# Where the last gate's modulation weights are loaded, and how gathered rows are spread, in a transformer block with a product-key expert layer

## Chip, cores and metric

The kernel runs on one core of one Trainium2 chip. The metric is device microseconds of one execution; three executions were timed.

## The reference

One block with 256 tokens and model width 2048: attention and pooling first, then an expert layer with 16384 experts, of which every token uses 128 (8 heads, 16 each). All is float32. Cut to what matters here:

```python
mod = jax.nn.silu(c) @ ada_w[layer] + ada_b[layer]          # 2048 x 12288
shift1, scale1, gate1, shift2, scale2, gate2 = jnp.split(mod[:, None, :], 6, axis=-1)
...
xn2 = rms_norm(h, norm2_g[layer]) * (1.0 + scale2) + shift2
h = h + gate2 * peer_ffn(xn2, peer_wq, peer_keys, peer_down, peer_up)
return rms_norm(h, final_g)

def peer_ffn(xn, w_query, sub_keys, w_down, w_up):
    q = jnp.einsum('bsd,de->bse', xn, w_query).reshape(B, S, 8, 2, 128)
    s = jnp.einsum('bshpd,hpnd->bshpn', q, sub_keys)
    top_s, top_i = lax.top_k(s, 16)
    ...                                                   # 16 of 256 pairs: expert, gates
    u = jnp.take(w_down, ic, axis=0)
    a = jax.nn.gelu(jnp.einsum('cd,ced->ce', xc, u), approximate=False) * gc
    return jnp.einsum('ce,ced->cd', a, jnp.take(w_up, ic, axis=0))
```

The last sixth of `mod` is `gate2`. It is used only when the expert layer's output is added.

## The kernel before

The work is a list of steps, each with one block of weights of 128 x 2048 (two loads of 128 x 1024 float32, 512 KB). `run` (from L292) goes over the list and emits the program. Weights come through five raw buffers in a fixed order: `want` notes the loads, `fill` issues one on the SP queue as soon as a buffer has been given back, `take` and `give` hand a buffer out and return it. In most steps ScalarE copies a raw tile to a rounded high part (L158, hi), VectorE subtracts to get the low part (L164, lo), which gives the raw buffer back, and TensorE multiplies with both parts. `plan` places these splits about one and a half steps ahead of the matmuls.

The modulation is not a matmul. `ada_half` (L211) takes a raw tile of `ada_w`, multiplies it on VectorE with the broadcast of silu(c) and sums along the row; a column of 128 outputs takes two such tiles. Steps have a list `ada` of the tiles they handle; the loads stand in the same queue.

The stages that the change touches come in this order:

- **Query steps** (16, `wq`): high and low split, scores, and the top-16 search on VectorE. POOL writes the normalized input beside it.
- **First down layer** (half 0, 64 steps, `down`): the hidden values of the first 8192 experts, for all of the 192 tokens that are computed against every expert. These steps are exact: TensorE takes the raw tile itself (L346) and gives it back after its 8 matmuls; there is no split. The routing (`route`) runs beside the first 24 steps on VectorE, then the gate matmuls (L1043) run beside the rest.
- **First up layer** (half 0, 64 steps, `up`): the output sums, split again, 20 matmuls a step (L1124, L1126, L1128). Before the change its first 32 steps each handle one of the 32 `ada` tiles of `gate2` (columns 80 to 95).
- **Second down layer** and **second up layer** (half 1): 64 steps each, both split (L181, L182 for down). At the start of the second down layer, a reload of hT, a load of the gate table A, the gate row for `gate2` and the residual sum (L1224, L1225) run beside it.

The other 64 tokens have their 128 experts' rows gathered, in 64 gathers of `down` rows and 64 of `up` rows, 128 rows of 8 KB (1 MB) each: POOL issues the gather (L1162) into one of two row buffers, VectorE multiplies and sums (L1173) or adds (L1180), and only then the gather after the next is issued. `share` gives each of the last steps of the first down layer (from step RS = 24) and of the three following layers a weight, and the 128 row steps are spread by the running sum:

```python
share = [0.75] * (HB - RS) + [0.35] * 32 + [0.55] * (HB - 32) + [0.5] * HB + [0.55] * (HB - 4)
```

which makes 31 row steps in the first down layer, 29 in the first up layer (11 of them in its first half), 33 in the second down layer and 35 in the second up layer.

Of the kernel before, what the change touches and what calls it, by code (L numbers as in the profile page):

```python
# [20 lines left out]
KC = D // P  # L21
# [6 lines left out]
HB = NB // 2  # L28
# [3 lines left out]
RS = 24  # L32
# [61 lines left out]
def peer_block_kernel(ctx: ExitStack, tc, xT_d, c_d, cols_d, const_d, ada_d, gates_d, wide_d, blk_d, mix_d, br_d,  # L94
# [151 lines left out]
    steps = []  # L246
# [46 lines left out]
    def run():  # L293
        for n, parts in plan():
            acts = parts[0] + parts[1]
            if n >= 0 and steps[n].exact:
                pre = int(n >= 1 and parts[0] != [] and parts[0][0][0] == "half")
                acts[pre:pre] = [("half", steps[n], i) for i in range(2)]
            for a in acts:
                if a[0] == "ada":  # L300
                    want(ada_d[a[1]][:, a[2] * HW:(a[2] + 1) * HW], HW)
                elif a[0] == "half" and (a[2] == 0 or a[1].w == D):
                    w = min(a[1].w, HW)
                    want(a[1].src[:, a[2] * w:a[2] * w + w], w)
        want(fg_d.unsqueeze(0).to_broadcast([P, D]))
        for n, parts in plan():
            s = steps[n] if n >= 0 else None
            if n >= 1:
                first = parts[0][0] if parts[0] else None
                if first and first[0] == "half":  # L310
                    parts[0][0] = first + (split_hi(first[1], first[2]),)
                if steps[n - 1].evac:
                    steps[n - 1].evac()
            if s:
                s.mm(s.hs, s.ls, 0)
                side_step(0)
                s.mm(s.hs, s.ls, 1)
                s.hs, s.ls = None, None
            for a in parts[0]:
                act(a)  # L320
            while late:
                late.popleft()()
            for _ in range(s.rows if s else 0):
                sparse_step()
            if s:
                side_step(1)
                if s.tick:
                    s.tick()
            for a in parts[1]:
                act(a)  # L330
        if steps[-1].evac:
            steps[-1].evac()
# [156 lines left out]
    n0 = len(steps)  # L489
# [10 lines left out]
    n0 = len(steps)  # L500
# [595 lines left out]
    def up_step(half, bl, oc):  # L1096


        hs = half_state[half]
        st = {}  # L1100

        def prep():
            assert hs["g"] == NG
            src = hs["A"][bl // AB][:, :, bl % AB, :]
            a = pp["pk2"].tile([P, 2 * ND], F32R, tag="a2", bufs=3, name="a2")
            nc.scalar.copy(a[:, :ND].rearrange("p (g u) -> p g u", u=TG), src)
            for n0, n, o in ((0, P, P + 2 * SP), (P, SP, ND)):
                nc.vector.tensor_sub(a[:, o:o + n].rearrange("p (g u) -> p g u", u=TG), src[:, n0 // TG:(n0 + n) // TG],  # L1108
                                     a[:, n0:n0 + n].rearrange("p (g u) -> p g u", u=TG).bitcast(F32))
            st["a"] = a  # L1110

        def mm(h_, l_, part):
            if bl == 0 and part == 0:
                oc.extend(psum(f"oc{i}") for i in range(8))
            a, last = st["a"], half == 1 and bl == HB - 1
            if last and part == 0:
                return

            def go(q, t, low):
                o, c = oc[2 * q + t], slice((q % 2) * 512, (q % 2 + 1) * 512)  # L1120
                w = (l_ if low else h_)[q // 2][:, c]
                st_, sp_ = bl == 0 and not low, low and bl == HB - 1
                if t:
                    nc.tensor.matmul(o, a[:, P:P + 2 * SP], w, start=st_, stop=sp_)  # L1124
                else:
                    nc.tensor.matmul(o, a[:, :P], w, start=st_, stop=sp_)  # L1126
                    if not low:
                        nc.tensor.matmul(o, a[:, P + 2 * SP:], w, start=False, stop=False)  # L1128

            if last:  # L1130
                order = [(q, t, low) for t in (1, 0) for q in range(4) for low in (False, True)]
            else:
                order = [(q, t, low) for low in (False, True) for q in (2 * part, 2 * part + 1) for t in range(2)]
            for o in order:
                go(*o)

        return Step(up_d[half * HB + bl], mm, after=[prep],
                    ada=[(80 + bl // 2, bl % 2)] if half == 0 and bl < 32 else [])

# [88 lines left out]
    for half in range(2):  # L1230
        n0 = len(steps)
        for bl in range(HB):
            steps.append(block_step(down_d[half * HB + bl], x2act if half else lambda k: x2f[:, k, :],
                                    lambda ps, half=half, bl=bl: h_done(half, bl, ps), both=half == 1, exact=half == 0))
        if half == 0:
            steps[n0 + 2].tick = open_late

            steps[n0 + 5].tick = lambda: side.append(gate_groups())
# [8 lines left out]
    steps[n0 + 24].tick = lambda: load_gates(NA - 1)  # L1247


    share = [0.75] * (HB - RS) + [0.35] * 32 + [0.55] * (HB - 32) + [0.5] * HB + [0.55] * (HB - 4)  # L1250
    total, seen = sum(share), 0.0
    for i, w in enumerate(share):
        n = int(seen / total * 2 * NP + 1e-6)
# [100 lines left out]
```

## Time and profile before

| | us |
|---|---|
| median of 3 executions | 2128.38 |
| lowest and highest | 2125.85, 2128.86 |
| profiled execution | 2129.82 |
| its span | 2127.9 |
| TensorE busy in the span | 1998.6 (94%) |
| VectorE busy in the span | 1683.0 (79%) |
| mean granted TensorE clock | 0.975 of 2.4 GHz |

The span is what the trace covers; the execution's own time is 1.9 us longer. Durations below come from this one execution. A busy share is a mean over stages with different limits, so a stage has to be read by itself. Issue to landing is the time from the instruction that issues a transfer to the semaphore that says it has landed.

### The profile page before, as it was taken

The page shows a single profiled execution, that of the slowest core. Times are in us where ns is not written, and L with a number is a line of the kernel's source. Part 1 is how long each engine was busy: PE and PEld are TensorE (multiplying, and loading weights), DVE is VectorE, ACT ScalarE, POOL GpSimd, SP SyncE. Part 2 cuts the span into 40 slices and gives each one's busy share as a digit, 9 for nine tenths or more (in the row PEclk, how much of TensorE's full clock was granted, in tenths as well). Part 3 has the DMA queues.
Part 4 walks back from the last instruction along what each step waited for, and adds up shares of the span by engine and source line. Part 5 has one row for each costly group of instructions (what it writes and reads, how often), then busy time and mean ns, then how long its engine had stood idle before and what let it go on. Part 6 is the DMA issues. An engine that isn't in the chain of part 4 may idle for free.

```text
span 2127.9 us, 33391 instructions
## 1 busy us (share of the span) xinstructions
PE 1998.6 (94%) x12444; PEld 1840.0 (86%) x12444; DVE 1683.0 (79%) x2908; ACT 900.9 (42%) x1473; POOL 368.4 (17%) x384
## 2 busy tenths in 40 slices
PE   7899999999999999999998878999689999999994
PEld 5889998999999999999996656878689999888883
DVE  8987887889888774577767767887588899888886
ACT  3344554544545411122224334454345556454553
POOL 2101231111216300111110000111111121332220
PEclk8999999999999999999999989999799999999997
DMA  9997877878986466899999999999879999999993
GB/s 373 380 341 259 317 266 246 283 276 311 316 306 197 143 205 200 315 324 319 329 331 317 310 318 328 372 360 351 254 268 334 349 354 359 350 359 353 352 362 112
DMA packets 171973, 648.83 MB, mean 305 GB/s; under 512 B 21025, under 2 KB 30529, under 8 KB 155041
## 3 DMA queue, kind: packets, MB, share of 16 engines
q1 hardware_dynamic: 147568, 499.18, 66.5%
q0 software_dynamic: 19200, 136.87, 17.5%
q10 hardware_dynamic: 5042, 10.64, 1.3%
q8 instruction: 98, 1.61, 0.3%
q14 instruction: 65, 0.53, 0.1%
HBM read 636.13 MB, written 10.49 MB: 304 GB/s over the span
## 4 chain that ended last, share of the span: by engine, by line
PE 62%; DMA 12%; DVE 9%; issue 4%; ACT 3%; POOL 0%; SPq 0%; DVEq 0%; ACTq 0%; POOLq 0%
PE blk L346 15%; PE oc L1124 8%; PE oc L1126 8%; PE blk L181 7%; DMA raw<-in_up_dram 7%; PE blk L175 4%; PE blk L176 4%; PE blk L174 4%; PE oc L1128 4%; DVE lo L164 3%; PE blk L182 3%; DMA raw<-in_blk_dram 2%; PE gps L1043 2%; ACT hi L158 2%; DVE raw L211 1%
## 5 line engine op out<-in xcount | busy, mean ns | idle before, releaser
L158 ACT CAST hi<-raw 128x1024 fp32r<-128x1024 f32 (+1 forms) x602 | 613.1, 1026 | 597.6 <-DMA raw<-in_up_dram 213.1
L164 DVE TENSOR_TENSOR lo<-raw,hi 128x1024 fp32r<-128x1024 f32 (+1 forms) x602 | 717.5, 1202 | 143.0 <-ACT hi L158 136.1
L346 PE MATMUL blk<-hT,raw 128*128 128x192 f32 x2048 | 338.0, 326 | 0.0
L346 PEld LDWEIGHTS blk<-hT,raw 128*128 128x128 f32 x2048 | 332.1, 190 | 0.5 <-issue 0.3
L181 PE MATMUL blk<-xn,hi 128*128 128x384 f32 x1024 | 302.2, 367 | 9.7 <-ACT hi L158 9.0
L182 PE MATMUL blk<-xn,lo 128*128 128x192 f32 x1024 | 260.6, 254 | 18.2 <-DVE lo L164 18.2
L211 DVE SCALAR_TENSOR_TENSOR raw<-raw,cb 128x1024 f32<-128x1024 f32 x165 | 213.0, 1309 | 40.5 <-DMA raw<-in_ada_dram 40.4
L1126 PE MATMUL oc<-hi,a 128*128 128x512 f32 x512 | 206.6, 404 | 33.2 <-ACT hi L158 33.2
L182 PEld LDWEIGHTS blk<-xn,lo 128*128 128x128 f32 x1024 | 199.2, 194 | 20.6 <-DVE lo L164 20.6
L1128 PE MATMUL oc<-hi,a 128*128 128x512 f32 x512 | 205.8, 402 | 4.8 <-DVE a L1108 4.7
L1124 PE MATMUL oc<-hi,a 128*128 128x512 f32 x512 | 205.5, 401 | 1.4 <-ACT hsum L1077 1.4
L1126 PE MATMUL oc<-lo,a 128*128 128x512 f32 x512 | 206.1, 403 | 0.0
L181 PEld LDWEIGHTS blk<-xn,hi 128*128 128x128 f32 x1024 | 195.9, 191 | 11.6 <-ACT hi L158 10.4
L1124 PE MATMUL oc<-lo,a 128*128 128x512 f32 x512 | 204.7, 400 | 0.0
L1162 POOL DMA_INDIRECT rows<-in_up_dram,spidx x64 | 125.5, 1962 | 441.9 <-DVE a L1108 200.1
L1162 POOL DMA_INDIRECT rows<-in_rows_dram,spidx x64 | 64.3, 1005 | 674.1 <-DVE a L1108 329.1
L1173 DVE SCALAR_TENSOR_TENSOR rows<-rows,rows 128x2048 f32<-128x2048 f32 x64 | 146.2, 2284 | 11.1 <-DMA rows<-in_rows_dram,spidx 11.1
L1126 PEld LDWEIGHTS oc<-hi,a 128*128 128x128 f32 x512 | 97.9, 191 | 61.5 <-ACT hi L158 38.5
L1180 DVE SCALAR_TENSOR_TENSOR rows<-rows,sph,rows 128x2048 f32<-128x2048 f32 x63 | 147.7, 2345 | 1.9 <-DMA rows<-in_up_dram,spidx 1.9
L174 PE MATMUL blk<-xna,hi 128*128 128x256 f32 x480 | 138.7, 289 | 0.0
L176 PE MATMUL blk<-xna,lo 128*128 128x256 f32 x480 | 135.8, 283 | 0.0
L175 PE MATMUL blk<-xna,hi 128*128 128x256 f32 x480 | 135.7, 283 | 0.0
(296 smaller groups left out, 3750.2 us busy)
## 6 DMA issues: line engine op xcount, KB each, us to landing
raw<-in_down_dram SPq DMA_DIRECT2D x256, 512.0 KB, 6.8
raw<-in_up_dram SPq DMA_DIRECT2D x256, 512.0 KB, 7.6
raw<-in_ada_dram SPq DMA_DIRECT2D x165, 512.0 KB, 5.8
raw<-in_blk_dram SPq DMA_DIRECT2D x80, 512.0 KB, 5.6
raw<-in_wout_dram SPq DMA_DIRECT2D x32, 512.0 KB, 5.9
raw<-in_wq_dram SPq DMA_DIRECT2D x32, 512.0 KB, 4.0
xraw<-in_ada_dram SPq DMA_DIRECT2D x27, 512.0 KB, 6.4
raw<-in_gates_dram SPq DMA_DIRECT2D x23, 512.0 KB, 5.7
```

The costliest lines, as they stand in the source:

```text
L158: nc.scalar.copy(hi, r)
L164: nc.vector.tensor_sub(lo, r, s.hs[i].bitcast(F32))
L174: nc.tensor.matmul(out, wh, ah, start=start, stop=False)
L175: nc.tensor.matmul(out, wh, al, start=False, stop=False)
L176: nc.tensor.matmul(out, wl, ah, start=False, stop=stop)
L181: nc.tensor.matmul(ps[:, :2 * ND], wh, a.rearrange("p s n -> p (s n)"), start=start, stop=False)
L182: nc.tensor.matmul(ps[:, :ND], wl, a[:, 0, :], start=False, stop=stop)
L211: nc.vector.scalar_tensor_tensor(raw, raw, 1.0, cb[:, i * HW:(i + 1) * HW], op0=ALU.mult, op1=ALU.mult, accum_out=modp[:, i, m:m + 1])
L346: nc.tensor.matmul(st["ps"][:, :ND], raw[:, c], a, start=k == 0, stop=k == KC - 1)
L1124: nc.tensor.matmul(o, a[:, P:P + 2 * SP], w, start=st_, stop=sp_)
L1126: nc.tensor.matmul(o, a[:, :P], w, start=st_, stop=sp_)
L1128: nc.tensor.matmul(o, a[:, P + 2 * SP:], w, start=False, stop=False)
```

## The change

It makes three edits. The 32 `ada` tiles of `gate2` move from the first 32 steps of the first up layer to the last 12 query steps and the first 20 steps of the first down layer, one a step. In exact steps the step's own two loads now always come first in the load order, and the early high-part split that came before them is left out there. And `share` has other weights: the first down layer now has 38 row steps, the first up layer 30, the second down layer 26 and the second up layer 34.

```diff
--- before.py
+++ after.py
@@ -294,8 +294,7 @@
         for n, parts in plan():
             acts = parts[0] + parts[1]
             if n >= 0 and steps[n].exact:
-                pre = int(n >= 1 and parts[0] != [] and parts[0][0][0] == "half")
-                acts[pre:pre] = [("half", steps[n], i) for i in range(2)]
+                acts[:0] = [("half", steps[n], i) for i in range(2)]
             for a in acts:
                 if a[0] == "ada":
                     want(ada_d[a[1]][:, a[2] * HW:(a[2] + 1) * HW], HW)
@@ -307,7 +306,7 @@
             s = steps[n] if n >= 0 else None
             if n >= 1:
                 first = parts[0][0] if parts[0] else None
-                if first and first[0] == "half":
+                if first and first[0] == "half" and not (s and s.exact):
                     parts[0][0] = first + (split_hi(first[1], first[2]),)
                 if steps[n - 1].evac:
                     steps[n - 1].evac()
@@ -1134,8 +1133,7 @@
             for o in order:
                 go(*o)
 
-        return Step(up_d[half * HB + bl], mm, after=[prep],
-                    ada=[(80 + bl // 2, bl % 2)] if half == 0 and bl < 32 else [])
+        return Step(up_d[half * HB + bl], mm, after=[prep])
 
 
 
@@ -1233,6 +1231,8 @@
             steps.append(block_step(down_d[half * HB + bl], x2act if half else lambda k: x2f[:, k, :],
                                     lambda ps, half=half, bl=bl: h_done(half, bl, ps), both=half == 1, exact=half == 0))
         if half == 0:
+            for m in range(2 * KC):
+                steps[n0 - 12 + m].ada.append((80 + m // 2, m % 2))
             steps[n0 + 2].tick = open_late
 
             steps[n0 + 5].tick = lambda: side.append(gate_groups())
@@ -1247,7 +1247,7 @@
     steps[n0 + 24].tick = lambda: load_gates(NA - 1)
 
 
-    share = [0.75] * (HB - RS) + [0.35] * 32 + [0.55] * (HB - 32) + [0.5] * HB + [0.55] * (HB - 4)
+    share = [0.95] * (HB - RS) + [0.47] * HB + [0.42] * HB + [0.55] * (HB - 4)
     total, seen = sum(share), 0.0
     for i, w in enumerate(share):
         n = int(seen / total * 2 * NP + 1e-6)
```

The changed program's line numbers are one lower from L299 on, two lower from L1138 on, and the same again from L1236 on.

**SP, the load queue, from the query steps on.** Before, the queue has all query loads, all down loads, and then one modulation tile after every two up loads:

```order
L132 DMA raw<-in_wq_dram 128x1024 x32
L132 DMA raw<-in_down_dram 128x1024 x126
L132 DMA raw<-in_up_dram 128x1024 x2
L132 DMA raw<-in_down_dram 128x1024 x2
L132 DMA raw<-in_up_dram 128x1024 x2
L132 DMA raw<-in_ada_dram 128x1024
L132 DMA raw<-in_up_dram 128x1024 x2
L132 DMA raw<-in_ada_dram 128x1024
L132 DMA raw<-in_up_dram 128x1024 x2
L132 DMA raw<-in_ada_dram 128x1024
```

After, from the last query steps into the first down layer:

```order
L132 DMA raw<-in_wq_dram 128x1024 x2
L132 DMA raw<-in_ada_dram 128x1024
L132 DMA raw<-in_wq_dram 128x1024 x2
L132 DMA raw<-in_ada_dram 128x1024 x2
L132 DMA raw<-in_down_dram 128x1024 x2
L132 DMA raw<-in_ada_dram 128x1024
L132 DMA raw<-in_down_dram 128x1024 x2
L132 DMA raw<-in_ada_dram 128x1024
L132 DMA raw<-in_down_dram 128x1024 x2
L132 DMA raw<-in_ada_dram 128x1024
L132 DMA raw<-in_down_dram 128x1024 x2
```

One modulation tile stands behind every two weight tiles from query step 4 to down step 19, and none in the up layer.

**SP, the up layer.** Before, around the first gate-table load (A):

```order
L132 DMA raw<-in_ada_dram 128x1024
L132 DMA raw<-in_up_dram 128x1024 x2
L132 DMA raw<-in_ada_dram 128x1024
L132 DMA raw<-in_up_dram 128x1024 x2
L1010 DMA A<-g2d 128x24x168
L132 DMA raw<-in_ada_dram 128x1024
L132 DMA raw<-in_up_dram 128x1024 x2
L132 DMA raw<-in_ada_dram 128x1024
L132 DMA raw<-in_up_dram 128x1024 x2
```

After, from the last modulation tile to the second gate-table load:

```order
L132 DMA raw<-in_ada_dram 128x1024
L132 DMA raw<-in_down_dram 128x1024 x86
L132 DMA raw<-in_up_dram 128x1024
L132 DMA raw<-in_down_dram 128x1024 x2
L132 DMA raw<-in_up_dram 128x1024 x52
L1009 DMA A<-g2d 128x24x168
L132 DMA raw<-in_up_dram 128x1024 x42
L1009 DMA A<-g2d 128x24x168
L132 DMA raw<-in_up_dram 128x1024 x33
```

The up loads run without anything between them but the two gate tables, and one up load stands before the last two down loads instead of two.

**VectorE, the routing of the second 64 tokens in the first down layer** (four, cp, tif, gz and e are routing tiles). Before, from the second top-16 search to the wait for ScalarE's exponential at gz:

```order
L860 MAX_INDEX cp<-four,tmpc 128x8 x4
L852 MAX four<-cand 128x8 x4
L854 MAX_INDEX cp<-four,cand 128x8 x4
L856 MATCH_REPLACE tmpc<-four,cand 128x50 x4
L858 MAX four<-tmpc 128x8 x4
L860 MAX_INDEX cp<-four,tmpc 128x8 x4
L933 TENSOR_TENSOR four<-four 128x128
L935 CAST four<-cp 128x128
L936 CAST tif<-tops 128x256
L937 COPY four<-tif 128x8
L938 TENSOR_TENSOR four<-tif 128x8x15
L941 TENSOR_REDUCE gz<-four 128x8
```

After, the same piece:

```order
L211 SCALAR_TENSOR_TENSOR raw,modp<-raw,cb 128x1024
L851 MAX four<-cand 128x8 x4
L853 MAX_INDEX cp<-four,cand 128x8 x4
L855 MATCH_REPLACE tmpc<-four,cand 128x50 x4
L857 MAX four<-tmpc 128x8 x4
L859 MAX_INDEX cp<-four,tmpc 128x8 x4
L932 TENSOR_TENSOR four<-four 128x128
L934 CAST four<-cp 128x128
L935 CAST tif<-tops 128x256
L936 COPY four<-tif 128x8
L937 TENSOR_TENSOR four<-tif 128x8x15
L211 SCALAR_TENSOR_TENSOR raw,modp<-raw,cb 128x1024
```

The modulation multiplies (L211) stand between the pieces of the routing, in program order.

## Rows read from the trace of the kernel before

**Rows 1.** The page: busy us by engine, then TensorE busy and clock in 40 slices.

```profile
PE 1998.6 (94%) x12444; PEld 1840.0 (86%) x12444; DVE 1683.0 (79%) x2908; ACT 900.9 (42%) x1473; POOL 368.4 (17%) x384
...
PE   7899999999999999999998878999689999999994
...
PEclk8999999999999999999999989999799999999997
```

**Rows 2.** Stretches: window, length, busy us (instructions) by engine, clock, DMA share, GB/s.

```profile
657.00:732.00 75.00, 75.00 (x636) 75.00 (x635) 57.82 (x225) 38.98 (x73) 40.26 (x61) 1.00 0.48 155
732.00:836.00 104.00, 104.00 (x646) 103.96 (x646) 69.50 (x351) 15.81 (x34) 1.14 (x2) 1.00 0.61 193
...
861.00:1110.00 249.00, 248.95 (x1651) 248.32 (x1649) 177.33 (x467) 54.21 (x249) 32.94 (x33) 1.00 0.91 325
1110.00:1320.00 210.00, 174.06 (x677) 133.64 (x676) 153.26 (x220) 77.78 (x100) 10.31 (x11) 0.93 0.90 317
1320.00:1466.00 146.00, 142.31 (x606) 113.21 (x604) 121.86 (x159) 74.04 (x94) 17.60 (x18) 1.00 0.98 368
1466.00:1600.00 134.00, 107.74 (x689) 104.41 (x690) 93.02 (x116) 55.65 (x88) 16.79 (x14) 0.90 0.83 278
```

**Rows 3.** Matmul lines L1128, L181, L1124 (from 1780 us): min/median/max ns, first and last start.

```profile
L1128 PE MATMUL oc<-hi,a x512: 392/396/792, 1110.2 to 2099.3; 128*128 128x512 f32 x171
...
L181 PE MATMUL blk<-xn,hi x1024: 354/361/686, 1466.5 to 1800.8; 128*128 128x384 f32 x171
...
L1124 PE MATMUL oc<-hi,a x256: 389/396/396, 1801.6 to 2096.5; 128*128 128x512 f32 x128
```

**Rows 4.** What the load queue SP waits for, 1110 to 1316 us: total, times, longest.

```profile
SPq L132 <- DVE lo L164: 97.6, 60, 8.6
...
SPq L132 <- DVE raw L211: 18.2, 12, 4.9
```

**Rows 5.** Raw loads issued in 1110 to 1320 us, from issue to landing.

```profile
DMA to landing us min/median/max: 4.0/7.2/13.4
```

**Rows 6.** Stretches of 20 us in the first up layer.

```profile
1100.00:1120.00 20.00, 18.57 (x96) 16.18 (x95) 12.71 (x20) 7.31 (x14) 1.87 (x2) 1.00 0.96 354
...
1380.00:1400.00 20.00, 17.58 (x74) 13.40 (x73) 12.79 (x17) 8.78 (x12) 1.87 (x2) 1.00 0.93 346
...
1440.00:1460.00 20.00, 20.00 (x88) 16.09 (x87) 17.25 (x22) 10.83 (x14) 1.87 (x2) 1.00 0.99 374
```

**Rows 7.** VectorE's wait in the query steps (657 to 732 us), and line L211.

```profile
DVE qT L872 <- ACT qsh L871: 13.1, 11, 1.5
...
L211 DVE SCALAR_TENSOR_TENSOR raw<-raw,cb x165: 1208/1218/2172, 11.5 to 1314.0; 128x1024 f32<-128x1024 f32 x165
L211 DVE DVE_READ_ACCUMULATOR raw<-raw,cb x165: 71/80/85, 13.6 to 1315.1; 128x1 f32 x165
```

**Rows 8.** Line L346, the exact matmuls of the first down layer.

```profile
L346 PE MATMUL blk<-hT,raw x2048: 325/326/430, 731.8 to 1109.8; 128*128 128x192 f32 x187
```

**Rows 9.** Raw loads issued in 735 to 855 us, from issue to landing.

```profile
DMA to landing us min/median/max: 3.6/4.2/5.2
```

**Rows 10.** Raw loads issued in 500 to 600 us, from issue to landing.

```profile
DMA to landing us min/median/max: 3.9/5.7/7.4
```

**Rows 11.** VectorE's waits in 732 to 861 us.

```profile
DVE gz L941 <- ACT four L934: 29.4, 2, 25.7
```

**Rows 12.** Gathered rows in 861 to 1107 us: the multiply, and issue to landing.

```profile
L1173 DVE SCALAR_TENSOR_TENSOR rows<-rows,rows x31: 2277/2283/2293, 872.7 to 1105.2; 128x2048 f32<-128x2048 f32 x31
...
DMA to landing us min/median/max: 7.0/9.0/12.5
```

**Rows 13.** DMA issues in 1801 to 2097 us: count, size, median us to landing.

```profile
rows<-in_up_dram,spidx POOLq DMA_INDIRECT x33, 10.4
```

**Rows 14.** Waits in 1466 to 1600 us.

```profile
DVE acc L1224 <- DMA g2b<-g2row: 15.9, 1, 15.9
```

**Rows 15.** VectorE's waits in 861 to 1107 us.

```profile
DVE A L1055 <- PE gps L1043: 47.8, 40, 4.9
```

## The prediction

> **What bounds the kernel now.** I read the page first. TensorE is busy for 94% of the span, and its digits below 9 lie, but for the start and the end, in slices 22 to 25 and 29 to 30, where the granted clock falls too [rows 1]. A mean over the program says nothing about a change that moves work between stages, so the second view is the table of stretches. It has the query stage, the first down layer (its first 20 steps, then the steps that take gathered rows), the first up layer cut at 1320 us, and the first 134 us of the second down layer [rows 2]. The reader should see three things in it. The first down layer is TensorE's: 104.00 of 104.00 us and 248.95 of 249.00 us busy. The first up layer loses time only in its first part: 174.06 of 210.00 us at a clock of 0.93, against 142.31 of 146.00 us afterwards. And DMA is lightly used just before: 155 GB/s in the query stage and 193 GB/s in the first 20 down steps.
>
> The third view is the source lines of the two up layers, which do the same matmuls. The first runs from its first matmul at 1110.2 us to the first matmul of the next layer at 1466.5 us, 356.3 us; the second from 1801.6 to 2099.3 us, 297.7 us, for the same 64 steps [rows 3]. The fourth view says why. In 1110 to 1316 us the load queue (SP) stands 97.6 us waiting for the low-part subtractions on VectorE and 18.2 us for the modulation multiplies on raw, that is, for one of five raw buffers to be given back [rows 4]. Three loads a step turn five buffers over too fast for landing times of 7.2 us [rows 5], so the stage runs at the pace of its loads.
>
> **Part 1: 32 modulation loads leave the first up layer.** They are 32 x 512 KB. Without them the layer has the loads of the second up layer, two a step, and 30 gathered rows, where the second one takes 35. So I take its 297.7 us as the model and add what the second one doesn't have: two gate-table loads (A from g2d, 2016 KB each) and the start. One such load fell in 1380 to 1400 us, where TensorE was busy for 17.58 of 20.00 us, so 2.4 us each; the start cost 20.00 - 18.57 = 1.4 us [rows 6]. That makes 297.7 + 4.8 + 1.4 = 303.9 us, a gain of 52 us. Bounds: the layer's own second part did 606 matmuls in 146.00 us [rows 2], so 1280 (20 a step) would take 308 us, a gain of 48; the undisturbed window had 88 in 20.00 us [rows 6], 291 us and a gain of at most 64 if nothing else disturbs it. The two layers' like shape decides for 52. The half-clock matmuls of this stretch, where the granted clock of 0.93 mixes the 1.2 and 2.4 GHz levels, are inside the 356.3 us; once TensorE no longer stands they go too.
>
> **Part 2: 12 of the loads enter query steps 4 to 15.** DMA has room (0.48 busy). VectorE is the question: each multiply takes 1.218 us plus a read of 0.08, which is 1.30 us more in a step of about 6.3 us. In the 75 us shown it is busy for 57.82 us [rows 2], so 12 x 1.30 = 15.6 us bring it to 73.4 of 75: full, but not over. What makes room is the wait of qT for the previous step's end, 13.1 us in 11 times [rows 7], which shrinks as VectorE runs later. The subtractions that TensorE needs are done about one step ahead, so a lag of a microsecond reaches nobody. I take 0, with 0 to +4 us.
>
> **Part 3: 20 of the loads enter the first 20 down steps.** Here TensorE uses the raw tile itself, as a step of 5.2 us (16 matmuls of 326 ns [rows 8]), and gives it back half a step later. With two loads a step, the first tile of a step was issued two steps ahead. With three in five buffers, it goes into the buffer that the step before last gave back, and has only 5.2 us from there to its use. Today loads in this stretch land in 4.2 us, at most 5.2 [rows 9]: no stall. But three in 5.2 us ask for 302 GB/s, and at 500 to 600 us, where modulation loads run between the others, the median is 5.7 us [rows 10], 0.5 us over the step or 10 us in 20 steps; the median with gathers beside them, 7.2 us [rows 5], would be 40 us. There are no gathers here yet, and the load issued just before is half a step older and nearly landed, so I stay near 4.2 to 5.2 and take 0.1 us a step: +2 us, with 0 to +10. VectorE has room: it is busy for 69.50 of 104.00 us [rows 2], 3.5 us a step and 4.8 with the multiply, under 5.2; and the routing runs so far ahead of TensorE today that it stands 25.7 us at one place for an exponential on ScalarE [rows 11]. If that cover were gone, each multiply that comes late would hold its raw buffer and so a down tile.
>
> By the Trainium skill (DMA: Bandwidth & Descriptors, section Anatomy of one DMA) a transfer issued by GpSimd costs about 2.0 us plus bytes over 436 GB/s, which for 512 KB is an estimate of 3.2 us; taken for these loads, the stall would be nothing and the sum 2 us lower. No landing in the rows is that short, and the rows decide.
>
> **Part 4: gathered rows.** 128 of them are spread by weights: now 31, 29, 33, 35 over the four layers, then 38, 30, 26, 34. In the first down layer 7 more mean 7 x 2.36 = 17 us on VectorE, which is busy for 177.33 of 249.00 us, and 7.3 MB on top of 325 GB/s, some 354 GB/s; the first up layer carries 368 today [rows 2]. The two row buffers turn over in (9.0 landing + 2.3 multiply) / 2 = 5.7 us at the median [rows 12], and at the 10.4 us median of the second up layer [rows 13] in 6.4 us; 38 rows in 249 us ask for one in 6.55. It just fits: 0 us. At the worst landing, 12.5 us, it would be 7.4 us, 0.85 x 38 = 32 us in all, if VectorE's lag reached TensorE. In the second down layer 7 fewer rows fall, 3 of them in the first 20 steps, where VectorE sets the pace after a wait of 15.9 us for the gate row [rows 14]; 3 x 2.36 = 7 us of its work, of which I count 3, bounds 0 and 7. The gate row itself is asked for behind a gather of the same step as now, so that wait stays. The second up layer keeps its rows but one.
>
> **Part 5: the order at the last exact step.** One up load now comes behind the last two down tiles and isn't split early; the first up step has 2.3 us more before it needs it. 0 us, up to +1.
>
> **Sum.** -52 + 0 + 2 + 0 - 3 + 0 = -53 us: span 2127.9 to 2074.9. The profiled execution took 2129.8 us, so 2076.8; it lies 1.4 us above the median of the runs shown, 2128.4, from which the same sum gives **2075 us**.
>
> **Rivals.**
> - *Landing time takes over in the first down layer.* The 20 steps run at the landing time instead of 5.2 us. At 5.7 to 6.2 us that costs 10 to 20 us in place of 2, so 2083 to 2093 us. For it: the median at that rate [rows 10]; against it: the one in this stretch [rows 9].
> - *The two row buffers take over in steps 24 to 63.* Half of the worst case, 16 us: 2091 us. For it: only 0.2 us of room at 10.4 us; against it: VectorE stood 47.8 us there waiting for TensorE's gate matmuls [rows 15], so a late row is first paid from that.
> - *Slower than before.* The first rival's mechanism at its full price: the gain of 53 us and the 2 already counted are gone when each of the 20 steps costs 2.75 us, which is a landing of 7.95 us. At 8.2 us the time is 2075 - 2 + 20 x 3.0 = 2133 us. Three loads a step do land in 7.2 us at the median and 13.4 at most today [rows 5], but beside gathers, and in a queue that VectorE holds up.
> - *No change.* If the first up layer's loss were VectorE's or the clock's own, taking the loads out would leave 2128 us. Against it: the part of the same layer without them is 97% busy.
> - *More.* The second down layer's first 134 us hold 26 us of idle TensorE [rows 2]; if fewer gathers there free 10 us more, 2065 us.
>
> **Numbers.** Forecast 0.66, with 2063 to 2087 us of its own; landing 0.12; row buffers 0.08; more 0.08; no change 0.02; slower 0.04. The range from 2061 to 2095 us takes in the bounds of part 1 (48 to 64) and most of the first two rivals; what it leaves out is somewhat under 2 in 10. A measurement of this kernel tells 0.2%, some 4 us, from no change: faster 0.94, same 0.02, slower 0.04.
>
> **What would show it.** Right: the first up layer lasts 300 to 308 us with the clock at 1.00 and no modulation loads; the query stage stays at 100% TensorE; the first 20 down steps take 104 to 106 us. Wrong: TensorE waits on raw loads in the first down layer with landings over 5.2 us; VectorE waits on gathered rows after step 24, with TensorE's gate matmuls behind it; the first up layer still stands on its load queue at two loads a step.

## The result, and the profile after

The changed kernel took 2094.99 us (median of 4 runs, 2086.04 to 2100.28), the kernel before 2128.62 beside it. The ratio is 0.984, with an interval of 0.980 to 0.988: 33.6 us faster. Of the executions in this document one, of 3937 us, with the spread of the rows alone, was far slower than the others and isn't in its ratio. The forecast was 2075 us, so 20 us of the expected 53 are missing, and the time lies at the very end of the range, 0.01 us inside its 2095. The profiled execution took 2096.6 us, against 2129.8 before. In its trace the line of the third up matmul is now L1127, that of the exact matmul L345.

The lines of the page that answer to [rows 1]: busy us by engine, then TensorE and its clock in 40 slices.

```profile
PE 1990.5 (95%) x12444; PEld 1837.9 (88%) x12444; DVE 1683.5 (80%) x2908; ACT 902.6 (43%) x1473; POOL 375.7 (18%) x384
...
PE   7899999999999998899999999998799999999994
...
PEclk7999999999999999999999999999899999999997
```

TensorE's weak slices 22 to 25 have gone, as forecast; those of the second down layer's start are now 28 and 29. New are two eights in slices 16 and 17, at 786 to 890 us: early steps of the first down layer, which were full before. Where each stage starts is read from its first matmul, as in [rows 3, 8]; of the changed kernel:

```profile
L345 PE MATMUL blk<-hT,raw x2048: 325/326/402, 731.7 to 1127.6; 128*128 128x192 f32 x187
...
L1127 PE MATMUL oc<-hi,a x512: 392/396/628, 1128.0 to 2065.7; 128*128 128x512 f32 x171
...
L181 PE MATMUL blk<-xn,hi x1024: 357/361/687, 1431.8 to 1767.2; 128*128 128x384 f32 x171
...
L1123 PE MATMUL oc<-hi,a x256: 392/396/396, 1768.0 to 2062.9; 128*128 128x512 f32 x128
```

| stage, us | before | after | difference | forecast |
|---|---|---|---|---|
| up to the first down layer | 731.8 | 731.7 | 0 | 0 |
| first down layer | 378.4 | 396.3 | +17.9 | +2 |
| first up layer | 356.3 | 303.8 | -52.5 | -52 |
| second down layer | 335.1 | 336.2 | +1.1 | -3 |
| second up layer, to its last L1124 or L1123 | 294.9 | 294.9 | 0 | 0 |

The missing time is nearly all in one stage. The stretches of the changed kernel, with the columns of [rows 2], show where in it:

```profile
657.00:732.00 75.00, 75.00 (x635) 75.00 (x634) 71.14 (x249) 38.98 (x74) 51.76 (x61) 1.00 0.76 239
732.00:836.00 104.00, 94.77 (x573) 91.72 (x572) 71.35 (x327) 14.96 (x32) 1.14 (x2) 1.00 0.75 248
861.00:1110.00 249.00, 249.00 (x1650) 248.98 (x1650) 187.97 (x484) 49.74 (x238) 37.39 (x37) 1.00 0.94 344
1128.00:1432.00 304.00, 301.32 (x1281) 241.14 (x1280) 242.52 (x315) 152.84 (x196) 33.02 (x31) 0.99 0.94 345
```

In 732 to 836 us TensorE issued 573 matmuls where it issued 646 before; from 861 us on it is full, gathered rows and all. The query steps are full too. What this stretch waited for, from the waits of the changed kernel in 735 to 855 us (total, times, longest):

```profile
SPq L132 <- DVE raw L211: 41.2, 8, 6.8
SPq L132 <- DVE ge L956: 22.2, 4, 7.2
...
PE blk L345 <- DMA raw<-in_down_dram: 14.2, 12, 3.2
...
DVE raw L211 <- DMA raw<-in_ada_dram: 40.9, 17, 5.0
```

Its raw loads issued there, from issue to landing, for [rows 9] (4.5 us at the median for the modulation tiles alone):

```profile
DMA to landing us min/median/max: 4.0/6.0/9.5
```

TensorE waits for down loads; the load queue waits for VectorE's modulation multiplies, or for the routing instruction that stands right behind one; VectorE waits for modulation loads. So the queue and VectorE wait for each other in turn, and the chain of waits in 770 to 830 us goes round between them (start, length, what; "DVE raw" is the multiply):

```profile
787.94 1.23 DVE raw L211 x2
789.17 0.03 DVE ge L956
789.20 6.82 DMA raw<-in_ada_dram
796.01 0.02 issue
796.04 1.25 DVE raw L211 x2
797.28 0.02 issue
797.30 4.81 DMA raw<-in_ada_dram
802.11 0.02 issue
802.14 1.23 DVE raw L211 x2
803.37 0.03 DVE ge L956
803.40 4.99 DMA raw<-in_ada_dram
```

Load, multiply, next load, multiply: no two of them overlap. From the first to the last of the 19 multiplies that start in 735 to 855 us (737.5 to 853.3) one takes 115.8 / 18 = 6.4 us, and TensorE's step is 5.2. The queue's own timeline shows what stands behind each modulation load:

```profile
797.30 0.33 SPq L132 DMA_DIRECT2D raw<-in_ada_dram  x1
797.72 0.87 SPq L132 DMA_DIRECT2D raw<-in_down_dram  x2
803.40 0.33 SPq L132 DMA_DIRECT2D raw<-in_ada_dram  x1
803.82 0.86 SPq L132 DMA_DIRECT2D raw<-in_down_dram  x2
```

The two down loads of a step go out only when the modulation load ahead of them has got its buffer.

Why a modulation load should wait for the modulation multiply just before it is told by the buffers. The source asks for "a raw buffer"; which of the five it is, the build decides. The addresses in the built program, in the order of the load queue, of the changed kernel and of three of the experiments below:

```
load            ada    down   down   ada    down   down   ada    down   down   ada
changed kernel  81376  77280  93664  81376  89568  85472  81376  77280  93664  81376
fixed rotation  93664  77280  81376  85472  89568  93664  77280  81376  85472  89568
own buffers    118240  81376  77280 126432  93664  89568 122336  85472  81376 114144
short multiply  85472  77280  85472  93664  89568  93664  81376  77280  81376  85472
```

In the changed kernel all 20 modulation tiles of these steps share the one buffer at 81376, and the down tiles rotate over the other four. The other rows are taken up below: a small edit makes the build hand the buffers out in another order.

### The profile page after: what moved, and what is told of

Read it like the earlier page. It is cut to its first block, busy times and chain, and to the rows that moved or that the text cites. A ratio compares the mean times of both kernels' runs of the same rounds, so it can differ in the third digit from the quotient of the medians.

```text
span 2094.7 us, 33340 instructions
## 1 busy us (share of the span) xinstructions
PE 1990.5 (95%) x12444; PEld 1837.9 (88%) x12444; DVE 1683.5 (80%) x2908; ACT 902.6 (43%) x1473; POOL 375.7 (18%) x384
## 3 DMA queue, kind: packets, MB, share of 16 engines
q0 software_dynamic: 19200, 136.87, 17.9%
## 4 chain that ended last, share of the span: by engine, by line
PE 66%; DMA 12%; DVE 8%; issue 3%; ACT 2%; POOL 0%; DVEq 0%; ACTq 0%; SPq 0%; POOLq 0%
PE oc L1123 11%; PE oc L1125 11%; PE blk L345 11%; PE oc L1127 6%; PE blk L181 5%; DMA raw<-in_ada_dram 5%; PE blk L175 4%; PE blk L174 4%; PE blk L176 4%; DMA raw<-in_down_dram 3%; PE blk L182 2%; DMA raw<-in_blk_dram 2%; PE gps L1042 2%; DVE lo L164 2%; DVE raw L211 2%
## 5 line engine op out<-in xcount | busy, mean ns | idle before, releaser
L345 PE MATMUL blk<-hT,raw 128*128 128x192 f32 x2048 | 341.0, 327 | 15.2 <-DMA raw<-in_down_dram 15.2
L345 PEld LDWEIGHTS blk<-hT,raw 128*128 128x128 f32 x2048 | 331.8, 190 | 19.0 <-issue 11.3
L181 PE MATMUL blk<-xn,hi 128*128 128x384 f32 x1024 | 304.2, 369 | 9.3 <-ACT hi L158 8.6
L211 DVE SCALAR_TENSOR_TENSOR raw<-raw,cb 128x1024 f32<-128x1024 f32 x165 | 212.4, 1306 | 45.3 <-DMA raw<-in_ada_dram 45.0
L181 PEld LDWEIGHTS blk<-xn,hi 128*128 128x128 f32 x1024 | 196.8, 192 | 10.6 <-ACT hi L158 9.3
L1123 PE MATMUL oc<-hi,a 128*128 128x512 f32 x512 | 203.0, 397 | 1.9 <-ACT hsum L1076 1.9
L1127 PE MATMUL oc<-hi,a 128*128 128x512 f32 x512 | 203.2, 397 | 0.1
L1125 PE MATMUL oc<-hi,a 128*128 128x512 f32 x512 | 203.1, 397 | 0.0
L1125 PE MATMUL oc<-lo,a 128*128 128x512 f32 x512 | 202.9, 396 | 0.0
L1123 PE MATMUL oc<-lo,a 128*128 128x512 f32 x512 | 202.7, 396 | 0.0
L1171 DVE SCALAR_TENSOR_TENSOR rows<-rows,rows 128x2048 f32<-128x2048 f32 x64 | 146.2, 2284 | 25.6 <-DMA rows<-in_rows_dram,spidx 25.5
L1123 PEld LDWEIGHTS oc<-hi,a 128*128 128x128 f32 x512 | 96.5, 188 | 25.5 <-ACT hsum L1076 2.3
```

The costliest lines, as they stand in the source:

```text
L181: nc.tensor.matmul(ps[:, :2 * ND], wh, a.rearrange("p s n -> p (s n)"), start=start, stop=False)
L211: nc.vector.scalar_tensor_tensor(raw, raw, 1.0, cb[:, i * HW:(i + 1) * HW], op0=ALU.mult, op1=ALU.mult, accum_out=modp[:, i, m:m + 1])
L345: nc.tensor.matmul(st["ps"][:, :ND], raw[:, c], a, start=k == 0, stop=k == KC - 1)
```

## The experiments

Theory A: this chain through one buffer sets the pace. Theory B: three loads in 5.2 us are too much for the transfers (the first rival of the prediction). Theory C: five buffers are too few for three loads a step, whichever way they are handed out. The layer times below are those of the profiled execution, measured as in the table above. The runs were timed in four sets, each beside the kernel before (medians of 2128.7 to 2133.4 us), so between sets the ratios compare better than the times.

**Own buffers.** The modulation tiles of this layer go into the low-part buffers, at most two handed out at a time. In the built program they go round all four of those buffers (the table above), not two, as the expectation says:

```diff
+            if o:
+                raw = wst.tile([P, HW], F32, tag="lo", bufs=HL_BUFS, name="adab")
+                own += 1
...
-                    want(ada_d[a[1]][:, a[2] * HW:(a[2] + 1) * HW], HW)
+                    want(ada_d[a[1]][:, a[2] * HW:(a[2] + 1) * HW], HW, a[1] >= 86)
```

> The 20 modulation tiles of the first down layer go into two of the low-part buffers, which stand idle in that layer; their place on the load queue stays. Theory A, a serial chain: each modulation tile waits for the buffer of the modulation tile before it, so its load (4.8 us), its multiply (1.25 us) and the next load follow one another every 6.05 us or more, with the two down loads of the step behind it on the same queue. Then the layer falls from 396 to 378 to 382 us and the time from 2095 to about 2078 us (2075 to 2082). Theory B, the rate of three loads in 5.2 us: as many bytes, the landing stays at 6 us, the layer at 393 to 398 us and the time at 2092 to 2097 us.

Measured: 2077.69 us (2073.35 to 2079.1), ratio 0.976 (0.974 to 0.978); the first down layer took 377.9 us. The stretch of 732 to 836 us, then the load queue's longest total of waits and the modulation tiles' landing in 735 to 855 us:

```profile
732.00:836.00 104.00, 104.00 (x646) 103.96 (x646) 83.67 (x361) 15.67 (x33) 1.14 (x2) 1.00 0.85 285
```

```profile
SPq L139 <- PE blk L353: 88.9, 44, 2.4
```

```profile
DMA to landing us min/median/max: 4.9/6.1/7.7
```

A's chain is gone and its number holds. The loads go at 285 GB/s in place of 248, the modulation tiles land in 6.1 us at the median, later than TensorE's step is long, and TensorE loses nothing: the queue waits for hardly anything but TensorE's giving buffers back. The rate, and B with it, is out.

**The same five buffers in a fixed rotation.**

```diff
-                raw = wst.tile([P, HW], F32, tag="raw", bufs=RAW_BUFS, name="raw")
+                raw = wst.tile([P, HW], F32, tag=f"raw{slot % RAW_BUFS}", bufs=1, name="raw")
+                slot += 1
```

> The same five raw buffers, but handed out in a fixed rotation, so that a modulation tile no longer gets the buffer of the modulation tile before it. A: the chain is broken; the layer takes 380 to 386 us, the time 2079 to 2086 us (the first tile of a step now has one step for its landing). B, and a theory C that five buffers are simply too few for three loads a step: the layer stays at 393 to 398 us, the time at 2092 to 2097 us.

Measured: 2082.13 us (2080.66 to 2083.54), ratio 0.978 (0.976 to 0.980); the layer 382.4 us. TensorE still waits for down loads, but little:

```profile
PE blk L346 <- DMA raw<-in_down_dram: 2.0, 6, 0.6
```

C is out: five buffers do, at +4.0 us. This is the handing out that the prediction had assumed, and the price is within its bounds of 0 to +10.

**A short multiply.** 64 columns in place of 1024.

```diff
+        w = 64 if m >= 86 else HW
-        nc.vector.scalar_tensor_tensor(raw, raw, 1.0, cb[:, i * HW:(i + 1) * HW], ...
+        nc.vector.scalar_tensor_tensor(raw[:, :w], raw[:, :w], 1.0, cb[:, i * HW:i * HW + w], ...
```

> The modulation multiplies of the first down layer take 64 of the 1024 columns (the sums of these 20 tiles leave out the other 960), so each lasts some 0.15 us in place of 1.23; loads and buffers stay. A: the chain's period falls from 6.05 to about 5.0 us, under the step of 5.2; the layer takes 379 to 385 us, the time 2078 to 2084 us. B: the transfers are the same, 393 to 398 us and 2092 to 2097 us. C, too few buffers: between them, some 388 us and 2087 us.

Measured: 2090.59 us (2086.02 to 2090.93), ratio 0.981 (0.979 to 0.983); the layer 390.4 us. A miss: a third of what A said. The multiply fell to 0.23 us, but the modulation loads now took 5.4 us at the median and not 4.5. The queue's wait in 735 to 855 us, then its timeline:

```profile
SPq L132 <- DMA raw<-in_ada_dram: 76.9, 19, 5.3
```

```profile
775.44 0.55 SPq L132 DMA_DIRECT2D raw<-in_ada_dram  x1
776.08 5.42 SPq L132 DMA_DIRECT2D raw<-in_down_dram  x2
781.59 0.38 SPq L132 DMA_DIRECT2D raw<-in_ada_dram  x1
```

This isn't the changed kernel's chain with a shorter link, for the build handed the buffers out anew. Soon after the start of the layer the modulation tiles go round three buffers, and the second down load of a step takes the buffer of the modulation tile just before it (85472 after 85472 in the table above). That down load waits until the modulation tile has landed and been multiplied, and the next modulation load stands behind it on the queue. So there is a chain again, by way of a down tile, and with 5.4 + 0.23 us and the issues it stays over 5.2. How much of the 17.9 us hangs on the multiply's length in the changed kernel is not shown.

**Another queue.** The 20 loads issued by GpSimd.

```diff
-                    want(ada_d[a[1]][:, a[2] * HW:(a[2] + 1) * HW], HW)
+                    want(ada_d[a[1]][:, a[2] * HW:(a[2] + 1) * HW], HW, nc.gpsimd if a[1] >= 86 else None)
```

> The 20 modulation loads of the first down layer are issued by GpSimd on its own queue; the buffers are the same five. A, with the queue's order as the link by which the chain reaches TensorE: the down loads no longer stand behind a modulation load that waits for a multiply, so the layer takes 379 to 384 us and the time is 2077 to 2083 us, while modulation tiles still follow one another at 6 us or more. If the single buffer alone were the cause, the layer stays over 390 us. B: 393 to 398 us and 2092 to 2097 us.

Measured: 2079.53 us (2075.01 to 2083.69), ratio 0.977 (0.976 to 0.979); the layer 381.3 us. The number is A's, but it doesn't prove the link it was meant for: the build handed the buffers out anew, and from the fourth on the modulation tiles went round three of them, in the pattern of the run before. For that pattern the two runs say that the queue's order is the link: with the modulation loads off the queue the layer took 381.3 us, though the multiply was at its full length. The next two runs keep the tiles in one buffer.

**One buffer, down tiles with all five, load queue as before.**

```diff
-                raw = wst.tile([P, HW], F32, tag="lo", bufs=HL_BUFS, name="adab")
+                one = one or [wst.tile([P, HW], F32, tag="lo", bufs=HL_BUFS, name="adab")]
+                raw = one[0]
```

> As the kernel with two own buffers (2078 us, first down layer 377.5 us), but with one buffer for the 20 modulation tiles; the down tiles keep all five raw buffers, and the order on the load queue is unchanged. Theory A, one buffer and one queue in order: the chain of load, multiply and next load is back, and the down loads stand behind it: the layer takes 390 to 400 us, the time is 2090 to 2098 us, as in the changed kernel. Theory C, that the changed kernel had too few raw buffers: the down tiles have five here, so the layer stays at 378 to 382 us and the time at 2078 to 2082 us.

Measured: 2091.22 us (2090.18 to 2093.13), ratio 0.982 (0.978 to 0.985); the layer 393.2 us. In this run and the next a multiply also waits for the tile after its own and reads that one's weights; the chain has the same links. The layer took 15.3 us more than with the own buffers and 3.1 less than in the changed kernel, though the down tiles have five buffers here in place of four. So C is out for the changed kernel too: one buffer is too few for this stream. How few would do isn't shown; the own buffers were four.

**The same, issued by GpSimd.** The load in the run above becomes `(nc.gpsimd if o else nc.sync).dma_start(raw, src)`.

> As the run before, one buffer for the modulation tiles, but their loads are issued by GpSimd on its own queue. A: the modulation tiles still come one every 6 us or more, but the down loads stand behind nothing, so TensorE keeps its 5.2 us step: the layer 377 to 381 us, the time 2076 to 2082 us. If the chain slows the layer in another way (through VectorE's order, say), 388 to 398 us and 2088 to 2096 us.

Measured: 2101.91 us (2099.81 to 2107.34), ratio 0.988 (0.984 to 0.992); the layer 408.1 us, slower than with one queue, and beyond the rival's 388 to 398 us too. This is A's second miss, and the most telling run. Two stretches, then the waits in 735 to 865 us, then the chain:

```profile
735.00:803.00 68.00, 68.00 (x422) 68.00 (x422) 36.44 (x182) 9.77 (x21) 5.39 (x10) 1.00 0.80 264
803.00:831.00 28.00, 0.94 (x5) 0.38 (x3) 19.36 (x53) 0.00 (x0) 2.65 (x5) 0.55 0.38 123
```

```profile
PE rtp L989 <- issue: 25.5, 1, 25.5
PE rtp L989 <- DVE e L983: 1.7, 1, 1.7
```

```profile
823.02 3.92 DMA adab<-in_ada_dram
826.94 0.02 issue
826.96 1.23 DVE adab L221 x2
828.20 0.66 DVE e L976 x2
...
830.42 0.67 DVE e L983 x2
831.09 0.04 issue
831.13 0.69 PE rtp L989 x2
```

With the down loads free, TensorE ran at its own pace up to 803 us and then stood for 27 us at the transposes of the routing's result (rtp), which need VectorE's products e. The view puts 25.5 us of that down to "issue", but the first transpose started at 828.96 us, as e of L976 and L977 was done, and the second at 831.13, right after L983. VectorE ran the modulation multiplies between its routing pieces, in the order of the program, each of them waiting for a load of the same chain, now one in 7.3 us (736.4 to 874.5 for 20 multiplies). So the load queue was only one of two ways from the chain to TensorE. Without it the lag was not gone; it was collected and paid at once. The single buffer is the cause, here and in the run before; the queue is a carrier.

**Every second step.** The 20 tiles over 40 steps of the layer, with five raw buffers and one queue.

```diff
-                steps[n0 - 12 + m].ada.append((80 + m // 2, m % 2))
+                steps[n0 - 12 + m if m < 12 else n0 + 2 * (m - 12)].ada.append((80 + m // 2, m % 2))
```

> The changed kernel with its 20 tiles in every second step of the first down layer, so over 40 steps; five raw buffers and one queue as before. A: a chain of 6 us has 10.4 us per tile and costs nothing in the first 24 steps; the layer takes 378 to 383 us, the time is 2077 to 2083 us. Theory D, that modulation loads beside gathered rows (steps 24 to 39) bring back landings as in the first up layer of the kernel before: 0.5 to 1.5 us in each of 8 steps, 384 to 392 us and 2083 to 2091 us.

Measured: 2083.99 us (2082.32 to 2087.2), ratio 0.979 (0.975 to 0.983); the layer 386.3 us, theory D's number. The first 24 steps are clean, as A says (120.00 of 120.00 us busy in 735 to 855). But in this build the modulation tiles go round four of the five buffers, so the run doesn't tell the slack that A counted on from the other handing out. The loss comes where modulation and gathers meet, TensorE's wait for down loads in 861 to 1110 us:

```profile
PE blk L345 <- DMA raw<-in_down_dram: 5.8, 3, 4.0
```

The three down loads that it waited for landed 10.2 to 11.7 us after their issue, and the granted clock was 0.98 in 855 to 880 us, with the longest wait, and 0.94 in 880 to 900. Gathers without modulation cost TensorE nothing in the changed kernel (249.00 of 249.00 us).

**The spread of the rows, taken back.** On top of the own buffers, `share` as in the kernel before.

> The kernel with two own buffers, with the gathered rows spread as in the kernel before (31, 29, 33, 35 in place of 38, 30, 26, 34). The forecast's part 4, that the new spread gives 3 us in the second down layer and costs 0 in the first: 332.6 us there becomes 335 to 336, and the time 2080 to 2082 us. The rival, that the wait for the gate row sets that stretch and the spread gives nothing: 331 to 334 us, and 2076 to 2079 us.

Measured: 2079.4 us (2076.22 to 2084.49), ratio 0.976 (0.972 to 0.979). The runs overlap with those of the new spread (2073.35 to 2079.1), so this decides nothing. The other way round tells a little more:

**The spread alone, on the kernel before.**

> The kernel before with the new spread of the gathered rows alone (38, 30, 26, 34 in place of 31, 29, 33, 35); all modulation loads where they were. The forecast's part 4: 0 in the first down layer, 3 us less in the second one (335 becomes 332), so 0.15% faster than before. The rival: the second down layer's wait for the gate row sets that stretch, so 0, within 0.1%. Against both: the first up layer of the kernel before has its 32 modulation loads still, and one more gathered row there would cost up to 7 us (0.3% slower).

Measured: 2127.68 us (2122.52 to 2131.28), ratio 0.9984 (0.9969 to 0.9999), 3.4 us by the ratio, between 0.2 and 6.6. The size is the forecast's; its place isn't shown by this run, since the second down layer of the profiled execution took 335.6 us (335.1 before). All profiled executions of this document with the gate row in its old place lean to it: that layer took 335.1 to 339.4 us in the three kernels with the old spread and 330.5 to 337.5 in the nine with the new one, 3.8 us less at the mean, with a scatter of 7.

**The 12 tiles of the query steps alone,** 20 left in the up layer.

```diff
-                    ada=[(80 + bl // 2, bl % 2)] if half == 0 and bl < 32 else [])
+                    ada=[(80 + bl // 2, bl % 2)] if half == 0 and 12 <= bl < 32 else [])
...
+            for m in range(12):
+                steps[n0 - 12 + m].ada.append((80 + m // 2, m % 2))
```

> The kernel before with 12 modulation loads moved to the query steps and 20 left in the first up layer (its steps 12 to 31); spread of the rows as before. The forecast's part 2: the query stage still ends at 731 to 732 us. Part 1 by the load: 52 us for 32 loads, so 12 of them give 19.5 us and the time is 2107 to 2111 us with a first up layer of 335 to 339 us. If the layer's loss came with its first steps alone (the start, the gate load), it would give all or nothing: under 2090 or over 2120 us.

Measured: 2110.59 us (2106.89 to 2115.01), ratio 0.990 (0.988 to 0.993), as expected, and 19.7 us less than the kernel before beside it. The profiled execution splits it otherwise: the first up layer took 330.4 us, 25.9 less and not 19.5, and the second down layer 339.4, 4.3 more. The query stage was full (75.00 of 75.00 us in 660 to 735), though it ended 3.2 us later than before, for a delay from before it (322 matmuls in 560 to 600 us, where the kernel before had 339).

**The gate row earlier.** The change has the modulation complete in the first down layer, so the gate row need not wait for the second one. Own buffers, and the row summed and loaded in step 30 of the first up layer:

```diff
+    def gate_row():
+        ada_fix(80, 96)
...
+    steps[n0 - 34].tick = gate_row
     steps[n0 + 4].tick = lambda: side.append(residual())
```

> The kernel with two own buffers, and the gate row, which can now be asked for as soon as the first down layer is over, is summed and loaded in step 30 of the first up layer in place of step 4 of the second down layer. If VectorE's wait of 17.7 us for that row is what makes TensorE stand at 1460 to 1520 us (14.4 and 4.6 us of idle time in two of three windows of 20 us), the second down layer falls from 332.6 to some 316 to 322 us and the time from 2078 to 2062 to 2067 us. If the landing of the first down loads (15 us beside the reload of hT) sets the stretch, 328 to 333 us and 2074 to 2079 us.

Measured: 2065.14 us (2063.53 to 2071.41), ratio 0.969 (0.967 to 0.971). The second down layer fell from 333.1 to 321.1 us, but the first up layer, where the row is loaded now, rose from 302.1 to 311.3. The two profiled executions are 1.9 us apart (2073.35 us, the lowest with own buffers alone, and 2071.41, the highest here) where the medians are 12.5 apart, so the stages show only in part where the gain of the medians lies. The wait that went is that of [rows 14]; with own buffers alone it was, in 1440 to 1500 us:

```profile
DVE acc L1230 <- DMA g2b<-g2row: 17.7, 1, 17.7
```

and the layer's first 134 us, 107.74 us of TensorE in the kernel before [rows 2], are now

```profile
1422.00:1556.00 134.00, 122.22 (x813) 120.11 (x812) 104.75 (x126) 66.70 (x104) 13.92 (x11) 0.95 0.83 292
```

**And the reload of hT moved** into step 54 of the first up layer (`steps[n0 + 1].tick` becomes `steps[n0 - 10].tick`).

> The version with own buffers and the early gate row (2065 us), with the 2 MB reload of hT moved from step 1 of the second down layer to step 54 of the first up layer; that tile is free from the end of the first down layer on. If the reload beside the gate-table load is what holds the first down loads up (12 to 15 us to landing; 14 us of waits of the high-part copies for them), the second down layer falls from 320.6 us by 4 to 7 us and the first up layer pays 2.4 us, as for one gate-table load: 2060 to 2063 us. If the bytes cost the same wherever they fall: 2064 to 2067 us.

Measured: 2065.14 us (2063.42 to 2066.17), ratio 0.970 (0.969 to 0.972). In this kernel the reload overwrites one gate table that lies in the tail of hT, so the last step of the first up layer multiplies with other values; the work is the same. The first up layer took 311.9 us, about as in the run above. The second down layer of the profiled execution fell to 311.8 us from 321.1, but the median didn't move. No other stage gives those 9 us back: the profiled executions differ by 8 (2063.42 and 2071.41 us, the lowest of this run and the highest of the run above), so the stages compare two ends here, and whether the move gains anything isn't settled. The layout has to change before it can be made, and by the medians it isn't worth it.

## Why the prediction was right or wrong

The sign, and the bulk, were right; the time came out 20 us over the forecast. Sixteen of them are one term of the sum that was mis-sized, and whose mechanism was wrong (part 3); four are the second down layer (part 4). That 2094.99 us still lies inside the range, by 0.01 us, is luck: the range reached that far for other reasons.

- **Part 1, right:** -52.5 us for a forecast of -52. The second up layer was the right model: the layer ran at 301.32 of 304.00 us busy with two loads a step. That it fits within 1 us is partly luck, since the layer took between 301.1 and 305.8 us in the kernels below that leave it like this, but for one gathered row. (The upper bound of the gain, from 291 us, comes to 65 and not 64.) Whether the gain is spread evenly over the loads is open: 12 of the 32 gave 25.9 us of the layer's 52.5 in one profiled execution, but by the medians 19.7, their even share.
- **Part 2, right:** TensorE stayed full in the query steps. VectorE was busy for 71.14 of 75.00 us, where the working had come to 73.4.
- **Part 3, the step that failed:** "+2 us, with 0 to +10" was +17.9. The prediction let each first tile go "into the buffer that the step before last gave back", a rotation over five buffers. That was read out of `take` and `give`, which count buffers but don't choose them. The build gave all modulation tiles one buffer, so a load waited for the multiply on the tile before it, and the time per step was landing + multiply in series, 6.4 us, in place of either alone. With the assumed rotation the term was +4.0, inside its bounds; with four buffers of their own for the modulation tiles it was nothing. The sentence "each multiply that comes late would hold its raw buffer and so a down tile" had the right link, but it was made to hang on VectorE's cover, [rows 11], and not on the handing out.
- **Part 4, half right:** the 38 rows cost TensorE nothing in the first down layer, 249.00 of 249.00 us, though VectorE stood 25.5 us for rows; on the own buffers that layer took 377.9 us with the new spread and 378.0 with the old one. The 3 us of the second down layer did not show there (+1.1). Alone, the spread gave 3.4 us with an interval that almost reaches 0, and over all kernels that layer is 3.8 us shorter with it, within a scatter of 7; so the term is likely, but not shown. That the wait for the gate row stays was right (17.1 us in the changed kernel), and with the row loaded earlier that layer lost 12 us.
- **Part 5:** nothing seen of it; it was not tested by itself.
- **The rivals.** The time fell just beyond "landing time takes over", 2083 to 2093 us, but not by its mechanism: with own buffers modulation tiles land in 6.1 us and cost nothing. Here the landing time set the step only where the next load couldn't be issued until the tile before had landed and been used. The two row buffers did not take over.

By the Trainium skill (DMA: Bandwidth & Descriptors, section Anatomy of one DMA) a 512 KB transfer issued by GpSimd is an estimate of 3.2 us; with the multiply of 1.25 the chain would have taken 4.45 us, under the step, and cost nothing. The raw loads here, issued by SP, landed in 4.0 to 9.5 us, and the modulation loads that GpSimd issued in the run with another queue in 5.2 us at the median; the measurement decides. The advice of the Trainium skill to double-buffer (Trainium Kernel Development and Optimization, section Best Practices) agrees with the runs in its direction: 2091 us with one buffer for the stream, 2078 with four.

## What to carry to other kernels

Count buffers by stream, not in total: a ring of five can leave one stream a single buffer, and then load and use stand in series. Read the addresses in the built program before costing a wait on "the next free buffer", and read them again for every experiment: three of the runs above changed the order without meaning to. And when a queue holds work up because loads stand behind one that waits, freeing the queue need not help: here VectorE, which ran its program in order too, carried the same lag. Look for the second way first.

## What the runs showed of the hardware that was not expected

Three loads in 5.2 us, 285 GB/s, raised the down tiles' landing from 4.2 us [rows 9] to 5.0 at the median, and TensorE lost nothing. After 28 us in which TensorE was busy for 0.94 us, the mean granted clock of that stretch was 0.55, between the levels of 1.2 and 2.4 GHz; it was 0.69 in 831 to 840 us and 1.00 again in 840 to 855.
